# Expert slots of a two-layer diffusion backbone: from four of 128 rows to three, expert 0 at 64 rows and first

## The chip, the cores and the metric

The kernel runs on one core of a Trainium2 chip. The metric is the time of one execution on the device in microseconds (us). The engines are called as in the profile: PE is the matrix engine (PEld its weight loads), DVE the vector engine, ACT the scalar engine, POOL the general one, and SP issues the weight transfers.

## What is computed

A backbone of two layers works on 256 latent and 256 context tokens of width 1024. Each layer mixes the tokens and then applies a feed-forward part: a dense SwiGLU in the first layer, and in the second one a mixture of eight SwiGLU experts for the 256 latent tokens, two experts per token. The change touches the experts alone:

```python
def swiglu(h, w_gate, w_up, w_down):
    return (jax.nn.silu(h @ w_gate) * (h @ w_up)) @ w_down

def moe_swiglu(h, router_w, w_gate, w_up, w_down):
    logits = (h @ router_w).astype(F32)
    top_v, top_i = lax.top_k(logits, TOP_K)
    top_w = jax.nn.softmax(top_v, axis=-1)
    combine = jnp.sum(jax.nn.one_hot(top_i, N_EXPERTS, dtype=F32) * top_w[..., None], axis=-2)
    out = jnp.zeros(h.shape[:-1] + (w_down.shape[-1],), h.dtype)
    for e in range(N_EXPERTS):
        out = out + combine[..., e:e + 1].astype(h.dtype) * swiglu(h, w_gate[e], w_up[e], w_down[e])
    return out
```

The gate and up matrices are 1024 x 2816, the down matrix 2816 x 1024, all float32. With the reference's own inputs (seed 0) its router gives experts 0 to 7 these numbers of tokens: 58, 99, 56, 77, 60, 69, 36, 57.

## The kernel before

The last stage of the kernel works through eight **slots**. A slot s is one expert's work for at most `CAPS[s]` rows (tokens), and `RANKS[s]` says which expert it takes: experts are ranked on the chip by their numbers of tokens, most first, and expert 0 is put at rank 0 whatever its number (L1080). So slot 0 always holds expert 0, with 128 rows; slots 2, 4, 6 hold ranks 1 to 3 with 128 rows; slots 1, 3, 5, 7 hold ranks 4 to 7 with 64 rows. Tokens over a slot's rows are counted in `most`; if there are any, a branch at the end (L1343) runs all eight experts once more for them.

Every slot streams one expert's weights in 33 transfers of 1 MB (`load`, issued by SP): 22 for gate and up in six groups of columns, then 11 for down. The buffers are used in turn: three of `wpool`, four of the pool `mo`, and three pieces of the tiles `own` and `whole`, ten in all.

- A 128-row slot (`expert`) splits each half of a transfer into a high and a low part (`split`: ACT L346, then DVE L347) and does three matmuls of 512 columns for each 128 x 512 block: L1196 to L1198 for gate and up, L1232 to L1234 for down.
- A 64-row slot (`expert64`) splits nothing. It uses the float32 weights as they are and puts two matmuls side by side in the array: L1253 for gate and up, L1289 for down. After each group SiLU (ACT L1259), a product (DVE L1260) and transposes (PE L1265, `turned`) make the operand of the down part.

Slots go in pairs that share their selection of tokens. `pick` makes a matrix `oh` of zeros and ones on DVE (L1140). `gather` multiplies the normalised tokens `hn` with it, 32 matmuls of 192 columns (128 for the one slot and 64 for the other) on PE (L1147), and evacuates them on ACT and DVE to `xg` (128 rows, in two parts) and `xs` (64 rows). `scatter_rows` (L1167, L1169) makes the way back, and `scatter` (L1305, L1308) adds a slot's result to the tokens, half of it late, in the next slot. The pair's 128-row slot comes first, and the next pair's gather runs inside the down part of the 64-row slot (`early`). Ahead of slot 0 stand, one after the other, positions and counts (L1059 to L1072), the ranking on DVE (L1078 to L1113), `pick` and the first gather.

Engines run their instructions in the order in which a scheduler put them, so a waiting instruction holds those behind it on its engine.

Of the kernel before, what the change touches and what calls it, by code (L numbers as in the profile page):

```python
# [20 lines left out]
KD = 8  # L21
# [18 lines left out]
RANKS = (0, 4, 1, 5, 2, 6, 3, 7)  # L40
CAPS = (128, 64, 128, 64, 128, 64, 128, 64)
# [40 lines left out]
def host_layout(x, c, ctx, c_ctx, ada_w, ada_b, mix_norm_w, ffn_norm_w, w_in, hg_lb_logits, hg_norm_w,  # L82
# [101 lines left out]
    "slots": (3, 5, 8),  # L184
# [12 lines left out]
def tile_kernel(ctx: ExitStack, tc: tile.TileContext, xT, cT, cR, ada_w, w_in, w_br, w_out, ffn_gu, ffn_d, router,  # L197
# [117 lines left out]
    more = {"pool": None, "raw": 0, "sp": 0, "own": []}  # L315
# [5 lines left out]
    def take(kind, base):  # L321

        turn[kind] += 1
        own = more["own"] if kind == "raw" else []
        return wpool if turn[kind] % (base + more[kind] + len(own)) < base else more["pool"]

    def load(ap, n=2048):
        if more["own"]:
            j = turn["raw"] % (3 + more["raw"] + len(more["own"]))
            if j in PLAN["slots"]:  # L330
                turn["raw"] += 1
                r = more["own"][PLAN["slots"].index(j)]
                nc.sync.dma_start(r[:, :n], ap)
                return r
        p = take("raw", 3)
        r = p.tile([P, 2048], F32, tag="raw", name=nm("raw"), bufs=3 if p is wpool else more["raw"])
        nc.sync.dma_start(r[:, :n], ap)
        return r
# [725 lines left out]
    for t in range(2):  # L1064
        for q in range(2):
# [3 lines left out]
            V.scalar_tensor_tensor(lv, pqs[2 * t + q], r, hv.bitcast(F32), ALU.mult, ALU.subtract)  # L1069
    pp = pm((P, 3, NE))  # L1070
# [46 lines left out]
    xg = mt((2, KD, P), "xg", 1, F32R)
    whole = hpool.tile([P, 2, 2048], F32, tag="hhi", name="whole")
    xs = whole[:, 0, :512].rearrange("p (k c) -> p k c", k=KD)
    a64 = whole[:, 0, 512:].rearrange("p (g q c) -> p g q c", g=6, q=2)  # L1120
    more_buffers(mo, *PLAN["moe"])
    own = hpool.tile([P, 2, 2048], F32, tag="hlo", name="own")
    more["own"] = [own[:, 0], whole[:, 1], own[:, 1]]
    home = {}

    def home_of(s_):

        if s_ == 0:
            return 0
        if s_ not in home:  # L1130
            home[s_] = nc.values_load(num_i[0:1, s_:s_ + 1], engines=[mybir.EngineType.SP], min_val=0, max_val=NE - 1,
                                      skip_runtime_bounds_check_because="clamped to 0..7 before it is stored")
        return home[s_]

    def pick(pr):
        oh = mt((2, 2, P), "oh", 1, F32R)
        for t in range(2):
            for ee in range(2):
                e = 2 * pr + ee
                V.tensor_scalar(oh[:, t, ee], iota64 if ee else iota, pos_s[:, t, e:e + 1], sel_s[:, t, e:e + 1],  # L1140
                                ALU.is_equal, ALU.mult)
        return oh

    def gather(k, oh, turns):
        pg = pm()[:, :192]
        for n, (s_, t) in enumerate(PARTS):
            T.matmul(pg, hn[s_][:, t, k * P:(k + 1) * P], oh[:, t].rearrange("p e s -> p (e s)")[:, :192],  # L1147
                     start=n == 0, stop=n == 3)
        x = tpool.tile([P, 512], F32, tag="tmp", name=nm("x"))[:, :P]
        with tc.high_priority():  # L1150
            for o, src in ((x, pg[:, :P]), (xs[:, k], pg[:, P:])):
                if turns and k % 2:
                    V.tensor_scalar(o, src, a2[:, k, 0:1], sh2[:, k, 0:1], ALU.mult, ALU.add)
                else:
                    S.activation(o, src, AF.Identity, scale=a2[:, k, 0:1], bias=sh2[:, k, 0:1])
            S.activation(xg[:, 0, k], x, AF.Copy)
            V.tensor_tensor(xg[:, 1, k], x, xg[:, 0, k].bitcast(F32), ALU.subtract)

# [15 lines left out]
    def expert(e, oh, st, choose, early):  # L1174
        pr, ee = divmod(e, 2)
        at_ = home_of(e)
        if ee:
            return expert64(e, at_, oh, st, choose, early)
        xv = [xg[:, s_] for s_ in range(2)]
        aT, turn_ = [], []  # L1180
        for g in range(6):
# [57 lines left out]
    def expert64(e, at_, oh, st, choose, early):  # L1239


        aT, turn_ = {}, []
        for g in range(6):
# [3 lines left out]
            for u in range(2):  # L1247
                for c in range(8 // kc):
                    raw = load(moe[at_, 4 * g + 2 * u + c if g < 5 else 20 + u]).rearrange("p (k c) -> p k c", k=kc)
                    for k in range(kc):  # L1250
                        kk = kc * c + k
                        for h_ in range(2):
                            T.matmul(ps[64 * h_:64 * h_ + 64, u, :hw], xs[:, kk], raw[:, k, h_ * hw:(h_ + 1) * hw],  # L1253
# [8 lines left out]
            def turned(a=a, g=g, nt=hw // P):  # L1262
# [3 lines left out]
                o = a64[:, g]  # L1266
# [28 lines left out]
    def scatter(e, h_, pd, ws, oT):  # L1295
# [5 lines left out]
        for m in range(0, 4, 2):  # L1301
# [34 lines left out]
    more["own"] = []  # L1336
# [6 lines left out]
    with tc.If(n_most > 0):  # L1343
        for e in range(NE):
            oh = mt((2, P), "oh", 1)
            shp = mt((2,), "ws", 2)
            V.tensor_scalar(shp, pos[:, :, e], cape[:, e:e + 1], None, ALU.subtract)
            for t in range(2):
                V.tensor_scalar(oh[:, t], iota, shp[:, t:t + 1], sel[:, t, e:e + 1], ALU.is_equal, ALU.mult)
            xe = hpool.tile([P, KD, P], F32, tag="hhi", name=nm("xe"))  # L1350
            for k in range(KD):
                pg = pm()
                for n, (s_, t) in enumerate(PARTS):
                    T.matmul(pg[:, :P], hn[s_][:, t, k * P:(k + 1) * P].bitcast(F32), oh[:, t],
                             start=n == 0, stop=n == 3)
                S.activation(xe[:, k], pg[:, :P], AF.Identity, scale=a2[:, k, 0:1], bias=sh2[:, k, 0:1])
# [88 lines left out]
```

## Time and profile before

| | us |
|---|---|
| three runs: lowest, median, highest | 2143.81, 2148.07, 2153.55 |
| the profiled execution, its own time | 2144.67 |
| its span in the profile | 2142.8 |
| PE busy in the span | 2049.2 (96%) |
| DVE, ACT busy | 1304.7 (61%), 928.2 (43%) |
| expert slots, first matmul to last down matmul | 1441.83 to 2127.34 |

The span is the time from the first to the last instruction in the profile; the execution's own time is 1.9 us longer. Busy time of PE counts matmuls whose ends are modelled, so it is read together with the idle time ahead of its instructions. Times in the views are counted from the span's start.

### The profile page before, as it was taken

The page shows a single profiled execution, that of the slowest core. Times are in us where ns is not written, and L with a number is a line of the kernel's source. Part 1 is how long each engine was busy: PE and PEld are TensorE (multiplying, and loading weights), DVE is VectorE, ACT ScalarE, POOL GpSimd, SP SyncE. Part 2 cuts the span into 40 slices and gives each one's busy share as a digit, 9 for nine tenths or more (in the row PEclk, how much of TensorE's full clock was granted, in tenths as well). Part 3 has the DMA queues.
Part 4 walks back from the last instruction along what each step waited for, and adds up shares of the span by engine and source line. Part 5 has one row for each costly group of instructions (what it writes and reads, how often), then busy time and mean ns, then how long its engine had stood idle before and what let it go on. Part 6 is the DMA issues. An engine that isn't in the chain of part 4 may idle for free.

```text
span 2142.8 us, 34452 instructions
## 1 busy us (share of the span) xinstructions
PE 2049.2 (96%) x13828; PEld 1578.5 (74%) x13828; DVE 1304.7 (61%) x2363; ACT 928.2 (43%) x1427; POOL 35.3 (2%) x101
## 2 busy tenths in 40 slices
PE   6999999999989999999999999989999999999997
PEld 3777777777868878887778888878757856865863
DVE  6667457764455468634777777669618707915941
ACT  3653234323334222223755443348527616715831
POOL 0001000000000000000000000000000000000000
PEclk9999999999999999999999999989999999999999
DMA  8341423112262346322333222369999999999996
GB/s 322 107 168 70 158 79 118 41 61 79 103 250 98 132 162 250 137 68 81 113 122 119 99 104 93 142 240 351 369 421 421 381 419 418 370 398 420 378 382 257
DMA packets 66984, 455.36 MB, mean 213 GB/s; under 512 B 7681, under 2 KB 8193, under 8 KB 13953
## 3 DMA queue, kind: packets, MB, share of 16 engines
q1 hardware_dynamic: 64080, 447.58, 54.3%
q10 hardware_dynamic: 2736, 5.51, 0.8%
q8 instruction: 111, 1.82, 0.3%
q14 instruction: 57, 0.46, 0.1%
HBM read 452.01 MB, written 1.05 MB: 211 GB/s over the span
## 4 chain that ended last, share of the span: by engine, by line
PE 89%; DVE 4%; ACT 4%; DMA 2%; issue 1%; SPq 0%; DVEq 0%; ACTq 0%
PE pj L353 15%; PE pj L354 15%; PE pj L355 15%; PE pj L1253 7%; PE pm L1289 4%; PE pm L1234 2%; PE pm L1232 2%; PE pm L1233 2%; PE pj L1196 2%; PE pj L1197 2%; PE pj L1198 2%; PE pm L590 1%; PE pa L798 1%; PE pm L373 1%; PE po L1198 1%
## 5 line engine op out<-in xcount | busy, mean ns | idle before, releaser
L346 ACT ACTIVATE whi<-raw 128x1024 fp32r<-128x1024 f32 (+3 forms) x442 | 436.1, 993 | 563.6 <-PE pj L354 480.3
L347 DVE TENSOR_TENSOR wlo<-raw,whi 128x1024 fp32r<-128x1024 f32 (+3 forms) x442 | 497.6, 1140 | 207.4 <-ACT whi L346 196.9
L353 PE MATMUL pj<-hhi,whi 128*128 128x512 f32 (+1 forms) x1216 | 452.3, 373 | 11.0 <-ACT hhi L482 8.5
L355 PE MATMUL pj<-hhi,wlo 128*128 128x512 f32 (+1 forms) x1216 | 450.6, 371 | 0.4 <-DVE wlo L347 0.4
L354 PE MATMUL pj<-hlo,whi 128*128 128x512 f32 (+1 forms) x1216 | 449.6, 370 | 0.1
L353 PEld LDWEIGHTS pj<-hhi,whi 128*128 128x128 f32 x1216 | 231.3, 190 | 52.4 <-ACT hhi L482 11.6
L354 PEld LDWEIGHTS pj<-hlo,whi 128*128 128x128 f32 x1216 | 231.2, 190 | 38.4 <-issue 2.3
L355 PEld LDWEIGHTS pj<-hhi,wlo 128*128 128x128 f32 x1216 | 230.9, 190 | 37.9 <-issue 2.5
L1253 PE MATMUL pj<-raw,whole 128*64 128x256 f32 (+1 forms) x1088 | 114.4, 362 | 0.0
L1260 DVE TENSOR_TENSOR act<-act,pj 128x256 f32<-128x256 f32 (+1 forms) x24 | 9.6, 399 | 156.6 <-ACT act L1259 156.6
L1253 PEld LDWEIGHTS pj<-raw,whole 128*64 128x64 f32 x1088 | 73.6, 137 | 33.1 <-issue 2.5
L1259 ACT ACTIVATE act<-pj 128x256 f32<-128x256 f32 (+1 forms) x24 | 8.8, 366 | 144.3 <-PE pj L1253 144.3
L353 PE MATMUL pj<-yhi,whi 128*128 128x512 f32 (+1 forms) x192 | 66.7, 350 | 3.4 <-ACT yhi L508 3.1
L355 PE MATMUL pj<-ahi,wlo 128*128 128x512 f32 x176 | 69.2, 393 | 0.8 <-DVE wlo L347 0.8
L353 PE MATMUL pj<-ahi,whi 128*128 128x512 f32 x176 | 69.1, 393 | 0.0
L1232 PE MATMUL pm<-whi,ahi 128*128 128x512 f32 x176 | 69.0, 392 | 0.0
L1197 PE MATMUL pj<-whi,xg 128*128 128x512 f32 (+1 forms) x192 | 68.8, 359 | 0.0
L1233 PE MATMUL pm<-whi,alo 128*128 128x512 f32 x176 | 68.6, 390 | 0.0
L354 PE MATMUL pj<-alo,whi 128*128 128x512 f32 x176 | 68.5, 389 | 0.0
L1196 PE MATMUL pj<-whi,xg 128*128 128x512 f32 (+1 forms) x192 | 68.4, 356 | 0.1
L1234 PE MATMUL pm<-wlo,ahi 128*128 128x512 f32 x176 | 68.2, 390 | 0.0
L1198 PE MATMUL pj<-wlo,xg 128*128 128x512 f32 (+1 forms) x192 | 68.1, 354 | 0.0
(364 smaller groups left out, 3613.8 us busy)
## 6 DMA issues: line engine op xcount, KB each, us to landing
raw<-in_moe_dram SPq DMA_DIRECT2D x185, 1024.0 KB, 8.8
raw<-in_w_in_dram SPq DMA_DIRECT2D x58, 1024.0 KB, 4.9
own<-in_moe_dram SPq DMA_DIRECT2D x53, 1024.0 KB, 9.0
raw<-in_ada_w_dram SPq DMA_DIRECT2D x44, 1024.0 KB, 5.0
whole<-in_moe_dram SPq DMA_DIRECT2D x26, 1024.0 KB, 8.6
raw<-in_ffn_gu_dram SPq DMA_DIRECT2D x22, 1024.0 KB, 4.8
raw<-in_w_br_dram SPq DMA_DIRECT2D x12, 1024.0 KB, 4.9
raw<-in_ffn_d_dram SPq DMA_DIRECT2D x16, 704.0 KB, 4.1
```

Of the source, the lines that this page charges most:

```text
L346: S.activation(hi, src, AF.Copy)
L347: V.tensor_tensor(lo, src, hi.bitcast(F32), ALU.subtract)
L353: T.matmul(ps, whi(k), hhi(k), start=first and k == 0, stop=False)
L354: T.matmul(ps, whi(k), hlo(k), start=False, stop=False)
L355: T.matmul(ps, wlo(k), hhi(k), start=False, stop=last and k == n - 1)
L1196: T.matmul(ps[:, :w], xv[0][:, kk], hi[:, k], start=kk == 0, stop=False)
L1197: T.matmul(ps[:, :w], xv[1][:, kk], hi[:, k], start=False, stop=False)
L1198: T.matmul(ps[:, :w], xv[0][:, kk], lo[:, k], start=False, stop=kk == 7)
L1232: T.matmul(pd[h_], ahi, hi[:, k % 2], start=first, stop=False)
L1233: T.matmul(pd[h_], alo, hi[:, k % 2], start=False, stop=False)
L1234: T.matmul(pd[h_], ahi, lo[:, k % 2], start=False, stop=last)
L1253: T.matmul(ps[64 * h_:64 * h_ + 64, u, :hw], xs[:, kk], raw[:, k, h_ * hw:(h_ + 1) * hw], start=u + kk == 0, stop=u == 1 and kk == 7, tile ...
```

## The change

Slots become `CAPS = (128, 64, 128, 64, 128, 64, 64, 64)` with `RANKS = (1, 0, 2, 4, 3, 5, 6, 7)`. Expert 0 is slot 1, with 64 rows; ranks 1 to 3 are slots 0, 2 and 4, with 128 rows; ranks 4 to 7 have 64 rows. In each pair the odd slot runs first, so the order is 1, 0, 3, 2, 5, 4, 7, 6. Slot 1 uses the unranked `pos` and `sel` of expert 0, and its gather (64 columns) is written ahead of the counts and the ranking; the gather of slot 0 (128 columns) stands inside slot 1, after its first group. Later gathers run in the down part of the pair's 128-row slot, and `scatter_rows` is done in the odd slot.

The 64-row operands move into columns of `xts` and `cm` that are no longer used. That frees a piece of `whole`, so there are eleven buffers, in a fixed ring (`mmmmwww0123`: four of `mo`, three of `wpool`, four pieces). A fourth PSUM tile for the transposed tokens comes from the group `pj`, where before it waited for one of the three `pm` tiles. The branch for left-over tokens now asks for each expert whether it has any.

```diff
-RANKS = (0, 4, 1, 5, 2, 6, 3, 7)
-CAPS = (128, 64, 128, 64, 128, 64, 128, 64)
+RANKS = (1, 0, 2, 4, 3, 5, 6, 7)
+CAPS = (128, 64, 128, 64, 128, 64, 64, 64)
...
-    pqs = [pm((P, 4, P)) for _ in range(4)]
+    pqs = [pm((P, 4, P)) for _ in range(3)]
 
     def rows_of(m):
+        if m == 4:
+            pqs.append(pj((P, 4, P)))
...
+    xs = [xts[k // 4][:, 64 * (k % 4):64 * (k % 4) + 64] for k in range(KD)]
+    xs2 = [cm[:, 64 * k:64 * k + 64] for k in range(KD)]
+    a64 = [xts[2 + g][:, :256].rearrange("p (q c) -> p q c", q=2) for g in range(6)]
...
+    more.update(own=[own[:, 0], whole[:, 0], own[:, 1], whole[:, 1]], ring=PLAN["ring"])
...
+                ps_, se, o = (pos, sel, 0) if RANKS[e] == 0 else (pos_s, sel_s, e)
...
+    ohs = [pick(0, (1,))]
+    for k in range(KD):
+        gather(0, k, ohs[0], (1,), True)
     pp = pm((P, 3, NE))
     T.matmul(pp[:, 2], onev, sel[:, 0], start=True, stop=False)
...
-        for ee in range(2):
-            def choose():
-                if ee and pr < 3:
+        for ee in (1, 0):
+            def choose(g):
+                if ee and pr + g == 0:
+                    pick(0, (0,), ohs[0])
+                    for k in range(KD):
+                        gather(0, k, ohs[0], (0,))
+                if ee and g == PLAN["sg"]:
+                    st.update(zip(("ws", "oT"), scatter_rows(pr, ohs[pr])))
+                if not ee and pr < 3 and g == PLAN["pk"]:
                     ohs.append(pick(pr + 1))
 
             def ahead(k):
-                if ee and pr < 3 and 0 <= k < KD:
-                    gather(k, ohs[pr + 1], False)
+                if not ee and pr < 3 and 0 <= k < KD:
+                    gather(pr + 1, k, ohs[pr + 1])
...
+            n_rest = nc.values_load(rest_i[0:1, e:e + 1], min_val=0, max_val=256)
+            with tc.If(n_rest > 0):
+                tokens_left(e)
```

**PE ahead of the first slot.** Before (rows left out at "..." are more of the gather, L1147):

```order
L1059 MATMUL pm_13067<-sel_13054,cc 128x16
L1060 MATMUL pm_13067<-sel_13054,onev 128x8
L1071 MATMUL pm_13081<-sel_13054,onev 128x8
L1072 MATMUL pm_13081<-sel_13054,onev 128x8
L1147 MATMUL pm_13133<-oh_13128,hn_2119_13071 128x192
...
L1196 MATMUL po_13213<-whi_13216,xg_13125 128x512
```

With the change (L1110 is the gather, L1129 and L1130 the counts, L1263 the gate and up matmuls of a 64-row slot, eight for a transfer; at the first "..." stand gathers, at the second two more transfers of L1263, at the third more of the gather of 128 columns):

```order
L1060 MATMUL pm_13067<-sel_13054,cc 128x16
L1061 MATMUL pm_13067<-sel_13054,onev 128x8
L1110 MATMUL pm_13087<-oh_13084,hn_2119_13071 128x64
...
L1129 MATMUL pm_13135<-sel_13054,onev 128x8
L1130 MATMUL pm_13135<-sel_13054,onev 128x8
L1263 MATMUL pj_13181<-raw_13182,x_5578 64x256 x8
...
L1263 MATMUL pj_13181<-raw_13212,x_5580 64x256 x8
L1110 MATMUL pm_13227<-oh_13084,hn_2119_13071 128x128 x2
...
L1263 MATMUL pj_13299<-raw_13300,x_5578 64x256 x8
```

The counts, and with them the ranking, moved behind the gather of expert 0; the second gather moved into the first slot.

**PE in a down part with a gather.** Before it was that of a 64-row slot (L1289; L1147 is the gather, L1265 a transpose of the last group):

```order
L1289 MATMUL pm_14367<-whole 64x512 x4
L1147 MATMUL pm_14376<-oh_14271,hn_2119_13071 128x192 x2
L1147 MATMUL pm_14376<-oh_14271,hn_2120_13072 128x192 x2
L1265 MATMUL pm_14386<-cc,act_14364 128x128
L1289 MATMUL pm_14367<-raw_14374,whole 64x512 x4
```

With the change it is that of a 128-row slot (L1242 to L1244, on split weights `whi` and `wlo`):

```order
L1244 MATMUL pm_14225<-wlo_14279,ahi_13856 128x512
L1110 MATMUL pm_14290<-oh_14040,hn_2119_13071 128x192 x2
L1110 MATMUL pm_14290<-oh_14040,hn_2120_13072 128x192 x2
L1242 MATMUL pm_14225<-whi_14300,ahi_13956 128x512
L1243 MATMUL pm_14225<-whi_14300,alo_13957 128x512
L1244 MATMUL pm_14225<-wlo_14301,ahi_13956 128x512
```

The gather's four matmuls for each of eight blocks moved from between unsplit weights to between split ones.

**PE in the first group of a 64-row slot** (four transfers to a group). Before, in slots 3, 5 and 7, the transposes of the group (L1265) follow its own last matmuls:

```order
L1253 MATMUL pj_16748<-whole 64x256 x8
L1253 MATMUL pj_16748<-raw_16758,whole 64x256 x8
L1253 MATMUL pj_16748<-raw_16768,whole 64x256 x8
L1253 MATMUL pj_16748<-own,whole 64x256 x8
L1265 MATMUL pm_16801<-cc,act_16787 128x128 x2
```

With the change, in slots 1, 3, 5 and 7, one transfer of the next group (another `pj`) stands between them:

```order
L1263 MATMUL pj_15906<-raw_15907,x_5578 64x256 x8
L1263 MATMUL pj_15906<-raw_15917,x_5580 64x256 x8
L1263 MATMUL pj_15906<-raw_15927,x_5578 64x256 x8
L1263 MATMUL pj_15906<-raw_15937,x_5580 64x256 x8
L1263 MATMUL pj_15950<-raw_15951,x_5578 64x256 x8
L1275 MATMUL pm_15961<-cc,act_15947 128x128 x2
```

Counted over a slot's first five groups in this order, transposes that follow their own group's last matmul are 2 in slot 1 and 5 in each of slots 3, 5 and 7 before (17); now they are none in slot 1, 3 in each of slots 3, 5 and 7, and 5 in slot 6 (14).

## Rows read from the trace of the kernel before

**Rows 1.** The page, chain of waits that ended last, by engine.

```profile
PE 89%; DVE 4%; ACT 4%; DMA 2%; issue 1%; SPq 0%; DVEq 0%; ACTq 0%
```

**Rows 2.** Windows, slots 0 to 7: us, PE, PEld, DVE, ACT, POOL, PEclk, DMA, GB/s.

```profile
1441.83:1538.03 96.20, 96.06 (x464) 79.26 (x462) 86.73 (x92) 73.86 (x82) 0.00 (x0) 1.00 0.90 340
1538.03:1610.74 72.71, 69.01 (x533) 38.79 (x532) 10.23 (x26) 14.94 (x41) 0.00 (x0) 1.00 1.00 413
1610.74:1707.79 97.05, 96.53 (x470) 80.35 (x470) 88.57 (x92) 74.43 (x79) 0.00 (x0) 1.00 1.00 404
1707.79:1783.52 75.73, 69.21 (x532) 38.82 (x531) 10.32 (x26) 14.93 (x41) 0.00 (x0) 1.00 1.00 414
1783.52:1882.15 98.63, 98.10 (x471) 81.56 (x471) 88.67 (x92) 74.42 (x79) 0.00 (x0) 0.98 0.98 386
1882.15:1957.88 75.73, 69.21 (x532) 38.77 (x532) 10.33 (x26) 14.93 (x41) 0.00 (x0) 1.00 1.00 411
1957.88:2056.43 98.55, 98.02 (x471) 81.43 (x471) 87.66 (x88) 74.41 (x79) 0.00 (x0) 0.98 0.98 383
2056.43:2127.34 70.91, 65.81 (x508) 36.50 (x507) 7.31 (x16) 7.61 (x19) 0.00 (x0) 1.00 0.89 363
```

**Rows 3.** Timeline of PE, slot 7: start, us, what, [idle before <-releaser].

```profile
2086.53 1.90 PE L1253 MATMUL pj<-whole 128*64 128x256 f32 x16
...
2091.09 0.44 PE L1265 MATMUL pm<-cc,act 128*128 128x128 f32 x2 [0.94 <-DVE act L1260]
```

**Rows 4.** Groups of PE by line and shape, 1428 us to the end.

```profile
L1147 PE MATMUL pm<-oh,hn 128*128 128x192 f32 x128 | 24.0, 318 | 5.3 <-DVE most L1111 4.9
...
L1265 PE MATMUL pm<-cc,act 128*128 128x128 f32 x44 | 9.9, 299 | 16.0 <-DVE act L1260 16.0
...
L1169 PE MATMUL pm<-cc,oh 128*128 128x128 f32 x16 | 4.7, 307 | 0.0
...
L1167 PE MATMUL pm<-by,oh 128*128 128x1 f32 x32 | 4.5, 209 | 0.0
```

**Rows 5.** Windows: slot 7 until its last transfer is in; 100 us in slots 1 and 2.

```profile
2056.43:2121.40 64.97, 59.87 (x482) 34.66 (x482) 7.31 (x16) 7.61 (x19) 0.00 (x0) 1.00 0.97 396
1555.00:1655.00 100.00, 95.77 (x590) 63.63 (x587) 48.29 (x64) 48.01 (x74) 0.00 (x0) 1.00 1.01 421
```

**Rows 6.** Timeline of PE ahead of slot 0.

```profile
1428.54 0.58 PE L1059 MATMUL pm<-sel,cc 128*128 128x16 f32 x2 [2.21 <-issue]
1428.95 0.57 PE L1060 MATMUL pm<-sel,onev 128*128 128x8 f32 x2
...
1435.24 6.76 PE L1147 MATMUL pm<-oh,hn 128*128 128x192 f32 x32 [4.85 <-DVE most L1111]
```

**Rows 7.** Timeline of DVE ahead of slot 0.

```profile
1429.57 0.17 DVE L1061 TENSOR_SCALAR pos<-pm 128x16 f32<-128x16 f32 x1 [0.85 <-PE pm L1060]
...
1434.23 0.34 DVE L1140 TENSOR_SCALAR oh<-cc,by,by 128x128 fp32r<-128x128 f32 x1
```

**Rows 8.** Timeline of ACT: a gather's three evacuations.

```profile
1436.83 0.46 ACT L1155 ACTIVATE x<-pm,mods,coef 128x128 f32<-128x128 f32 x1 [9.68 <-PE pm L1147]
1437.19 0.40 ACT L1155 ACTIVATE whole<-pm,mods,coef 128x64 f32<-128x64 f32 x1
1437.48 0.31 ACT L1156 ACTIVATE xg<-x 128x128 fp32r<-128x128 f32 x1
```

**Rows 9.** Windows of 5 us: two with idle time of PE; a stretch in slot 4.

```profile
1425.00:1430.00 5.00, 2.55 (x11) 2.21 (x12) 3.75 (x14) 1.25 (x3) 0.00 (x0) 0.50 1.00 423
...
2080.00:2085.00 5.00, 4.06 (x36) 2.41 (x34) 0.42 (x1) 0.77 (x2) 0.00 (x0) 1.00 1.01 421
...
1784.82:1788.23 3.41, 3.41 (x8) 2.76 (x9) 2.85 (x3) 1.60 (x2) 0.00 (x0) 0.50 1.02 423
```

More of the change, by code (lines that the diff above doesn't have):

```diff
@@ L183 @@
     "td": 2,
-    "slots": (3, 5, 8),
+    "ring": "mmmmwww0123",
     "pk": 3,
@@ L312, in tile_kernel @@
     lb_v, lb_n = lb[:, 2], lb[:, 3]
-    more = {"pool": None, "raw": 0, "sp": 0, "own": []}
+    more = {"pool": None, "raw": 0, "sp": 0, "own": [], "ring": ""}
     turn = {"raw": 0, "sp": 0}
@@ L323, in take @@
         turn[kind] += 1
-        own = more["own"] if kind == "raw" else []
-        return wpool if turn[kind] % (base + more[kind] + len(own)) < base else more["pool"]
+        return wpool if turn[kind] % (base + more[kind]) < base else more["pool"]
     def load(ap, n=2048):
[L328 to L336, printed above, removed]
+        if more["ring"]:
+            kind = more["ring"][turn["raw"] % len(more["ring"])]
+            turn["raw"] += 1
+            p = {"w": wpool, "m": more["pool"]}.get(kind)
+            r = more["own"][int(kind)] if p is None else None
+        else:
+            p, r = take("raw", 3), None
+        if r is None:
+            r = p.tile([P, 2048], F32, tag="raw", name=nm("raw"), bufs=3 if p is wpool else more["raw"])
         nc.sync.dma_start(r[:, :n], ap)
@@ new lines, in tile_kernel, with home_of @@
+    own = hpool.tile([P, 2, 2048], F32, tag="hlo", name="own")
+    more_buffers(mo, *PLAN["moe"])
+    more.update(own=[own[:, 0], whole[:, 0], own[:, 1], whole[:, 1]], ring=PLAN["ring"])
+    turn["raw"] = 0
+    home = {}
+    def home_of(s_):
+        if RANKS[s_] == 0:
+            return 0
+        if s_ not in home:
+            home[s_] = nc.values_load(num_i[0:1, s_:s_ + 1], engines=[mybir.EngineType.SP], min_val=0, max_val=NE - 1,
+                                      skip_runtime_bounds_check_because="clamped to 0..7 before it is stored")
+        return home[s_]
@@ L1117, in tile_kernel @@
[L1117 to L1133, printed above, removed]
@@ L1135, in pick @@
-    def pick(pr):
-        oh = mt((2, 2, P), "oh", 1, F32R)
-        for t in range(2):
-            for ee in range(2):
[L1139 to L1157, printed above, removed]
+    V.tensor_copy(rest_i, cnt_)
@@ L1213, in expert @@
             turn_.append(turned)
-            if g == PLAN["pk"]:
-                choose()
+            choose(g)
             if g == PLAN["sg"]:
-                if late:
-                    late.pop()()
-                st.update(zip(("ws", "oT"), scatter_rows(pr, oh)))
+                late.pop()()
         pd = [pm(), pm()]
@@ L1319, in tile_kernel @@
     norm = Norm(256, lambda: pt("po", 1))
-    late, ohs = [], [pick(0)]
-    for k in range(KD):
-        gather(k, ohs[0], True)
+    late = []
     for pr in range(4):
         st = {}
-        for ee in range(2):
-            def choose():
-                if ee and pr < 3:
+        for ee in (1, 0):
[7 more added lines that the diff above has]
+                if not ee and pr < 3 and g == PLAN["pk"]:
@@ L1344, in tile_kernel @@
         for e in range(NE):
[L1345 to L1356, printed above, removed]
@@ L1387, in tile_kernel @@
-            pd = [pm(), pm()]
-            for c in range(11):
-                raw = load(moe[e, 22 + c]).rearrange("p (k c) -> p k c", k=4)
-                for k in range(4):
-                    h_, kk = DOWN[4 * c + k]
-                    first, last = (kk == 0, kk == 21) if h_ == 0 else (kk == 20, kk == 19)
-                    T.matmul(pd[h_], ae[:, kk], raw[:, k], start=first, stop=last)
-            y = mt((2, 512), "y")
-            for h_ in range(2):
-                S.activation(y[:, h_], pd[h_], AF.Copy, scale=ws[:, 0:1])
@@ L1397, in tile_kernel @@
-            yf = y.rearrange("p a b -> p (a b)")
-            ov = oT.rearrange("p t c -> p (t c)")
-            for m in range(KD):
-                ps = pm()
-                T.matmul(ps[:, :256], yf[:, m * P:(m + 1) * P], ov, start=True, stop=True)
-                V.scalar_tensor_tensor(xl[m], ps[:, :256], mods[1][:, 40 + m, 0:1], xl[m], ALU.mult, ALU.add)
+            n_rest = nc.values_load(rest_i[0:1, e:e + 1], min_val=0, max_val=256)
+            with tc.If(n_rest > 0):
+                tokens_left(e)
```

147 lines of the change are left out of this document (101 added, 46 removed).

## The prediction

> **What bounds the kernel now.** I read the chain of waits that ended last first: 89% of the span lies on PE and 2% on transfers [rows 1]. That is an average over stages, so the windows of the eight slots come next [rows 2]. Look at three columns there. PE: in each slot its busy time fills the window but for a few us. DVE and ACT: 87 to 89 and 74 us in a 128-row slot, about 10 and 15 in a 64-row slot. GB/s: 383 to 414 in slots 1 to 6. So a 128-row slot lasts 96 to 99 us for 33 transfers, a 64-row slot 71 to 76.
>
> How fast can transfers come? In 100 us with no hole they ran at 421 GB/s [rows 5]. A transfer is 1024 x 256 float32 or as many elements in another shape, 1.0486 MB, so 2.49 us each and 82 us for a slot's 33. A 128-row slot (2.9 to 3.0 us a transfer on PE) is slower than that, a 64-row slot (2.15 to 2.3) faster, and lives on what the ten buffers hold. Slots now alternate, so PE never runs dry. The idle time that PE does have is of one kind: 0.94 us ahead of a transpose, for the product on DVE [rows 3], 16.0 us over the stage [rows 4], 17 times.
>
> Where the trace is silent: no two 64-row slots follow each other, no gather stands between split matmuls, none is 64 columns wide.
>
> **The change, term by term.** I sum by pairs of slots, because the gather and `scatter_rows` only move within a pair or between its members. All is set against the profiled execution's own time, 2144.67; the median of the runs is 3.4 above that.
>
> *First three pairs.* Each stays one 128-row and one 64-row slot: 168.9, 172.8 and 174.4 us by the windows [rows 2]. The gather's matmuls move from a 64-row to a 128-row slot at the same cost on PE. Its evacuations move too: 0.46 + 0.40 + 0.31 = 1.17 us of ACT for each of eight blocks [rows 8]. ACT has 74 busy us of 97 there, so 9.4 more fit on average; and PE spends 4 x 0.18 = 0.72 us of each block on the gather itself, during which the next splits can run. I cost this at nothing; cover gone, it is a rival below. What changes for certain is the order of transposes: of 17 gaps 14 stay, and those of the first three pairs fall from 12 to 6 (slots 3 and 5 have 3 each, slot 1 none). 6 x 0.94 = **-5.6 us**.
>
> *Last pair.* It was 98.55 + 70.91 = 169.5 us [rows 2]; now both slots have 64 rows. PE's work: 2 x 70.91 plus `scatter_rows`, 16 matmuls of 4.7 us and 32 of 4.5 over four pairs [rows 4], so 2.3 a pair: 144.1. In this pair the gaps go from 5 in slot 7 to 5 in slot 6 and 3 in slot 7; 2 x 70.91 holds ten of them, so two go, -1.9: 142.2 us if PE never waits for weights.
>
> The transfers are slower than that. In the old slot 7 they ran 64.97 us at 396 GB/s until the last one was in [rows 5]: 25.7 MB or 24.5 transfers. So 8.5 of the 33 were in when it began, of ten buffers, and 24.5 x 2.49 = 61.0 leaves 4.0 us of holes. Now 66 transfers are wanted and eleven buffers put some 9.5 ahead, because the slot before the pair still has 128 rows and lets the ring fill. 56.5 x 2.49 + 4.0 = 144.7 us until the last one is in; its own matmuls take about 1.9 [rows 3]: 146.6. PE catches up with the transfers late in the second slot and waits some 4 us in all. 146.6 - 169.5 = **-22.9 us**.
>
> What the chip's memory gives is the number on which this rests. The rows say 421 GB/s over 100 us, 414 over a whole slot. The Trainium skill (DMA: Bandwidth & Descriptors, "Where 436 GB/s comes from") holds that in a transfer from memory into the on-chip buffer the memory side, some 358 GB/s, is what limits a core. By that figure 56.5 transfers would take an estimated 165.5 us and the pair 171.4, so the whole term would be lost, and the sum would be 2142. The trace disagrees with that for one core working alone [rows 2, 5]; I go by the trace.
>
> *Start.* Before, PE counts, waits 4.85 us for the ranking on DVE, gathers 192 columns in 6.76 us [rows 6], and slot 0 begins at 1441.83. Now expert 0 needs no rank: positions are out at 1429.57 + 0.17 = 1429.74, two picks at 0.34 follow [rows 7], and a gather of 64 columns can begin at 1430.4. The price of its 32 matmuls isn't shown. From above it is 6.76, that of 192 columns; from below a third of it, 2.3. The later gathers took (24.0 - 6.76)/96 = 0.18 us a matmul [rows 4, 6], in place of 0.21; I take 0.18, since for small shapes the duration hardly falls with the columns (209 ns for one column, 307 for 128 [rows 4]): 5.8 us, to 1436.2. The two count matmuls cost some 0.9 us (0.58 and 0.57 for their like, which overlap a little [rows 6]); the first slot begins at 1437.1, 4.7 earlier. The ranking then runs on DVE under a slot that leaves it idle. But the gather of 128 columns now stands inside that slot, another 32 x 0.18 = 5.8 us that was part of the 6.76 before. Together **+1 us**, between -5 (both gathers priced by columns) and +3.
>
> The clock could add to it. Between 1425 and 1430, PE busy for 2.55 of 5 us, the granted clock was 0.50, which is 1.2 of 2.4 GHz [rows 9]. The new start leaves PE less idle, which if anything helps.
>
> *Nothing.* The fourth tile of transposes moves ahead of the stage where PE is not held by it; the branch per expert adds eight tests of a number at the end in place of one, on engines that are done, below 1 us each, and no more than 1 to 2 us if they come one after the other: it is in the range. The eleventh buffer is in the term above.
>
> Sum: -22.9 - 5.6 + 1 = -27.5; 2144.67 - 27.5 = 2117.2, and 2120.6 if set against the median. I give **2118 us**.
>
> **The rivals.**
>
> *PE never waits (2113).* If the transfers' 4.0 us of holes vanish because eleven buffers in a fixed ring keep them fed, the pair takes 142.6, PE's own time or nearly: 4 us less. For it: 421 GB/s held over 100 us. Against it: the old slot 7, whose buffers were also free early, had the holes.
>
> *The evacuations hold the splits (2128).* ACT and DVE work through their queues in order, and the splits of the next weights stand behind a gather's evacuations. 1.17 us of ACT against 0.72 of PE leaves 0.45 us a block; 8 blocks in 3 slots make 10.7, so 2128. Fully exposed it is 3 x 9.4 = 28 us, and the gain is gone. For it: DVE is busy 87 of 97 us in such a slot [rows 2], and takes a part of these evacuations. Against it: PE has other split weights waiting in that time.
>
> *Transfers stay slow (2131).* With no 128-row slot in the pair the holes may not close: at the 383 GB/s of slot 6 [rows 2], 2.74 us each, 56.5 of them take 154.8, the pair 160.7, and the time is 2131. The skill's rule above would stand here, at 2142, with a small chance.
>
> *Slower: the clock halves.* In the last two slots PE waits for weights again and again. In a stretch where the granted clock was 0.50, eight 128 x 512 matmuls took 3.41 us, 0.43 each, against 96.53/470 = 0.21 in slot 2 [rows 2, 9]. With all of the last pair at that clock PE would need 284 us instead of 142, and the kernel 2255. The gain of 27.5 is used up once 32 us of the pair's work run at half clock (the first 4.4 lie under the wait for transfers). Against it: between 2080 and 2085 PE was busy for 4.06 of 5 us, and the clock stayed at 1.00 [rows 9]; waiting for weights would leave it busy for 1.9 of 2.49, which is as much to the eye. For it: the 0.50 at 2.55 of 5. The Trainium skill (TensorE: Matmul & The Clock Gate, "HAM oscillation — how this bites in real kernels") tells of just such a kernel, slowed to a half by waits for transfers between bursts of matmuls.
>
> *The branch for left-over tokens is taken (2215).* Expert 0 has 64 rows whatever its number. By the reference's counts it has 58, so 6 more would be needed; the branch decides at the 65th token and costs at least one expert's transfers, 33 x 2.49 = 82 us, and a second time what follows the slots, 2142.8 - 2127.3 = 15.5 us by the table of times.
>
> **How the numbers follow.** The forecast has 0.56, PE-bound 0.17, held splits 0.18, slow transfers 0.04, half clock 0.04, the branch 0.01. What a measurement of this kernel can tell from no change is about 0.5%, 10.7 us: faster means below 2137.3. That holds for the first three, and part of the fourth and of the clock's case: 0.91; within 0.5% 0.04; slower 0.05. The range reaches from 2105 (2113 with the start at its best end, -6, and 2 for the profile's distance) to 2131 (held splits and the start's bad end), which leaves out the rest.
>
> **What would show it.** Slot 1 first, beginning near 1437. Slots of 128 rows as long as before, with no idle time of PE ahead of L1242 where the gather stands. The last two slots together near 147 us, with PE's idle time ahead of L1263 or L1298 put down to transfers, only in the second slot; the transfers at 415 GB/s or more over both. The granted clock at 1.00 there. I would be wrong if the last pair took over 155 us, if gaps of PE after each gather add up to more than 5 us, or if the clock fell to 0.50.

## The result and the profile after

The changed kernel takes 2124.95 us (median of four runs, 2120.40 to 2126.47), beside 2147.41 before (also four runs): ratio 0.9889, with a 95% interval of 0.9861 to 0.9916, a gain of 22.5 us or 1.1%. The forecast was 2118 in 2105 to 2131. The profiled execution is the slowest of the four, 2126.47, with a span of 2124.7.

The chain of waits that ended last, by engine, in the kernel after, answers to [rows 1]:

```profile
PE 84%; DMA 6%; DVE 5%; ACT 3%; issue 2%; SPq 0%; DVEq 0%; ACTq 0%
```

Transfers went from 2 to 6% of the span. The windows of its slots, in the order 1, 0, 3, 2, 5, 4, 7, 6, and then of what follows them, answer to [rows 2] (same columns):

```profile
1437.88:1511.38 73.50, 71.03 (x537) 40.45 (x536) 13.84 (x54) 12.73 (x33) 0.00 (x0) 0.96 0.91 369
1511.38:1614.05 102.67, 102.15 (x491) 84.06 (x491) 89.91 (x95) 80.12 (x102) 0.00 (x0) 0.98 0.99 402
1614.05:1684.89 70.84, 65.90 (x512) 36.70 (x511) 9.16 (x23) 8.05 (x18) 0.00 (x0) 1.00 0.99 409
1684.89:1787.68 102.79, 102.26 (x490) 84.11 (x490) 89.88 (x95) 80.14 (x102) 0.00 (x0) 0.98 0.98 393
1787.68:1858.53 70.85, 65.90 (x513) 36.70 (x512) 9.17 (x23) 8.05 (x18) 0.00 (x0) 1.00 1.00 411
1858.53:1961.12 102.59, 102.06 (x490) 84.22 (x490) 88.34 (x87) 78.69 (x94) 0.00 (x0) 0.98 0.98 392
1961.12:2029.27 68.15, 64.93 (x512) 36.48 (x513) 7.37 (x17) 6.37 (x15) 0.00 (x0) 1.00 1.00 412
2029.27:2106.52 77.25, 67.61 (x509) 36.00 (x505) 7.30 (x16) 7.62 (x19) 0.00 (x0) 1.00 0.96 397
2106.52:2124.69 18.17, 5.07 (x17) 3.24 (x16) 5.66 (x13) 3.22 (x7) 0.00 (x0) 0.68 0.19 63
```

Read it by pairs. The last pair took 145.4 us where it had been 169.5. In its second slot PE is busy for 67.6 of 77.3 us, with the clock at 1.00: it waits for weights. Two of its waits (PE: start, us, what, idle before):

```profile
2071.30 1.95 PE L1263 MATMUL pj<-whole,cc 128*64 128x256 f32 x16 [0.54 <-DMA whole<-in_moe_dram]
...
2083.73 1.94 PE L1298 MATMUL pm<-raw,x 128*64 128x512 f32 x8 [0.55 <-DMA raw<-in_moe_dram]
```

Such waits add up to 4.1 us there; in the pair's first slot there is none. The other pairs got longer or hardly shorter: 176.2, 173.6 and 173.4 against 168.9, 172.8 and 174.4. And each 128-row slot shows a clock of 0.98.

The chain through the last pair, in order of time (start, us, what; pieces under 5 us left out):

```profile
2009.76 5.33 PE pm L1298 x24
...
2015.10 16.41 DMA raw<-in_moe_dram
...
2031.62 19.76 DMA raw<-in_moe_dram
...
2051.50 19.76 DMA whole<-in_moe_dram
...
2071.38 19.77 DMA raw<-in_moe_dram
...
2101.22 5.33 PE pm L1298 x24
```

A transfer takes 19.8 us from issue to landing here: eight are in flight, and they land 2.49 us apart. From 2015 to 2091 the chain holds nothing but transfers and their issue. From the pair's start to the last landing, and from there to the last down matmul (windows, columns of [rows 2]):

```profile
1961.12:2103.55 142.43, 129.56 (x1007) 71.76 (x1008) 14.67 (x33) 13.99 (x34) 0.00 (x0) 1.00 1.00 412
2103.55:2106.52 2.97, 2.97 (x14) 0.72 (x10) 0.00 (x0) 0.00 (x0) 0.00 (x0) 1.00 0.00 0
```

142.4 + 3.0 = 145.4, where the sum had 144.7 + 1.9 = 146.6.

Now the entry into a 128-row slot, here slot 2. First ACT, then PE (start, us, what, idle before):

```profile
1683.21 0.69 ACT L1308 ACTIVATE y<-pm,ws 128x512 fp32r<-128x512 f32 x1 [11.06 <-PE pm L1298]
1683.80 2.94 ACT L345 ACTIVATE whi<-raw 128x1024 fp32r<-128x1024 f32 x3
```

```profile
1684.89 0.50 PE L1209 MATMUL po<-whi,xg 128*128 128x512 f32 x1 [1.73 <-ACT whi L345]
...
1686.15 0.61 PE L1211 MATMUL po<-wlo,xg 128*128 128x512 f32 x1 [0.53 <-DVE wlo L346]
1686.56 0.63 PE L1209 MATMUL po<-whi,xg 128*128 128x512 f32 x1
```

ACT idles for 11 us at `y`, the late half of the 64-row slot's result, which needs PE's last down matmul; the splits of the next weights stand behind it. PE then waits twice, and its matmuls take 0.63 us in place of 0.39, as the granted clock has fallen to 0.50. The same gaps, 1.73 and 0.53 us, were in the kernel before at the entries of slots 2, 4 and 6; the granted clock fell behind two of them there, behind all three now.

The start of the experts on PE:

```profile
1428.40 0.58 PE L1060 MATMUL pm<-sel,cc 128*128 128x16 f32 x2 [5.03 <-issue]
...
1430.13 7.01 PE L1110 MATMUL pm<-oh,hn 128*128 128x64 f32 x32 [0.74 <-DVE oh L1102]
...
1437.88 8.46 PE L1263 MATMUL pj<-raw,x 128*64 128x256 f32 x64
1446.28 2.45 PE L1110 MATMUL pm<-oh,hn 128*128 128x128 f32 x20
```

The gather of 64 columns takes 7.0 us, all of it at clock 0.50; that of 192 columns took 6.8 [rows 6], most of it at 0.50. In that state the matmuls of both start 213 ns apart (median), so their count sets the price, not their width. The gather of slot 0's 128 columns stands at 1446, inside slot 1.

### The profile page after: what moved, and what is told of

Same layout as the page of the kernel before. It is cut to its first block, busy times and chain, and to the rows that moved or that the text cites. A ratio compares the mean times of both kernels' runs of the same rounds, so it can differ in the third digit from the quotient of the medians.

```text
span 2124.7 us, 34306 instructions
## 1 busy us (share of the span) xinstructions
PE 2029.1 (96%) x13901; PEld 1542.2 (73%) x13901; DVE 1220.6 (57%) x2280; ACT 856.1 (40%) x1357; POOL 35.3 (2%) x101
## 4 chain that ended last, share of the span: by engine, by line
PE 84%; DMA 6%; DVE 5%; ACT 3%; issue 2%; SPq 0%; DVEq 0%; ACTq 0%
PE pj L352 15%; PE pj L353 15%; PE pj L354 14%; PE pj L1263 8%; PE pm L1298 3%; DMA raw<-in_moe_dram 3%; PE pm L1242 1%; PE pm L589 1%; PE pm L1244 1%; PE pm L1243 1%; PE pj L1210 1%; PE pj L1211 1%; PE pj L1209 1%; DVE wlo L346 1%; PE pm L372 1%
## 5 line engine op out<-in xcount | busy, mean ns | idle before, releaser
L345 ACT ACTIVATE whi<-raw 128x1024 fp32r<-128x1024 f32 (+2 forms) x382 | 372.9, 982 | 544.8 <-PE pj L353 479.9
L346 DVE TENSOR_TENSOR wlo<-raw,whi 128x1024 fp32r<-128x1024 f32 (+2 forms) x382 | 426.4, 1127 | 211.3 <-ACT whi L345 206.5
L352 PEld LDWEIGHTS pj<-hhi,whi 128*128 128x128 f32 x1216 | 231.4, 191 | 53.6 <-ACT hhi L481 12.5
L353 PEld LDWEIGHTS pj<-hlo,whi 128*128 128x128 f32 x1216 | 231.4, 190 | 38.3 <-issue 2.3
L1263 PE MATMUL pj<-raw,x 128*64 128x256 f32 x896 | 104.1, 389 | 0.0
L1263 PEld LDWEIGHTS pj<-raw,x 128*64 128x64 f32 x896 | 64.1, 140 | 34.6 <-issue 5.4
L1309 DVE SCALAR_TENSOR_TENSOR y<-pm,ws,y 128x512 fp32r<-128x512 f32 x16 | 12.0, 750 | 98.4 <-ACT y L1308 98.4
L1298 PE MATMUL pm<-raw,x 128*64 128x512 f32 x280 | 64.1, 597 | 3.1 <-DMA raw<-in_moe_dram 3.1
L353 PE MATMUL pj<-ylo,whi 128*128 128x512 f32 (+1 forms) x192 | 66.3, 346 | 0.0
L354 PE MATMUL pj<-yhi,wlo 128*128 128x512 f32 (+1 forms) x192 | 66.2, 345 | 0.0
L1242 PE MATMUL pm<-whi,ahi 128*128 128x512 f32 x132 | 52.8, 400 | 0.0
L1308 ACT ACTIVATE y<-pm,ws 128x512 fp32r<-128x512 f32 x16 | 10.9, 684 | 103.2 <-PE pm L1298 93.1
```

The source lines that it names most:

```text
L345: S.activation(hi, src, AF.Copy)
L346: V.tensor_tensor(lo, src, hi.bitcast(F32), ALU.subtract)
L352: T.matmul(ps, whi(k), hhi(k), start=first and k == 0, stop=False)
L353: T.matmul(ps, whi(k), hlo(k), start=False, stop=False)
L354: T.matmul(ps, wlo(k), hhi(k), start=False, stop=last and k == n - 1)
L1242: T.matmul(pd[h_], ahi, hi[:, k % 2], start=first, stop=False)
```

## The experiments

All ran beside the kernel before on the same chip. Ratios are to the kernel before; the changed kernel's is 0.9889. The slots are compared by their lengths in the profiled executions: the work ahead of the experts, which only experiment 7 touches, ended anywhere from 1417.2 to 1423.1 us there, so whole times of two kernels can differ by some us for that alone.

**1. Slot 6 back to 128 rows** (`four128`).

```diff
-CAPS = (128, 64, 128, 64, 128, 64, 64, 64)
+CAPS = (128, 64, 128, 64, 128, 64, 128, 64)
```

> Slot 6 back to 128 rows (rank 6 gets them, after slot 7), everything else as in the changed kernel: this undoes the last pair's term alone. Theory (the last pair is where the time came from): the pair goes from 145.4 to some 168 to 170 us (64-row slot near 68, 128-row slot near 100, without a gather in it), and the end comes 23 to 25 us later: some 2149, no better than before the change, so that everything else in the change is worth nothing or less together. Rival (the order, the start and the buffers have a share in the gain): some 2138.

Measured: 2147.29 us, ratio 1.0004 (0.9990 to 1.0018). The last pair of `four128`, windows:

```profile
1959.64:2029.69 70.05, 65.10 (x512) 36.33 (x511) 8.14 (x19) 8.06 (x18) 0.00 (x0) 1.00 1.00 408
2029.69:2129.09 99.40, 98.87 (x466) 80.81 (x466) 87.93 (x87) 75.21 (x82) 0.00 (x0) 1.00 0.73 304
```

169.45 us against 145.40: 24.1 us, and the whole gain is gone. So the last pair accounts for the gain, and order, start, buffers and transposes together are worth nothing that can be measured.

**2. Eight buffers in place of eleven** (`ring8`).

```diff
-    "ring": "mmmmwww0123",
+    "ring": "mmmmwww0",
```

> The ring of buffers cut from eleven to eight (the last three pieces are not used); nothing else. Theory (the last pair is bound by transfers, so each buffer fewer is one transfer fewer ahead when the pair begins): 3 x 2.49 = 7.5 us later, some 2132, with PE's waits for transfers in the last pair starting in the first of its two slots. Rival (PE's own work bounds the pair, or the fixed order of the ring is what keeps the transfers fed): no change, 2125, or a loss spread over all slots.

Measured: 2136.35 us, ratio 0.9962 (0.9948 to 0.9976). The windows of slot 1 and of the last pair:

```profile
1431.94:1509.21 77.27, 71.89 (x536) 40.28 (x535) 13.83 (x54) 12.72 (x33) 0.00 (x0) 0.96 0.91 372
1958.37:2029.29 70.92, 65.75 (x513) 36.17 (x512) 7.38 (x17) 6.88 (x16) 0.00 (x0) 1.00 1.00 410
2029.29:2111.70 82.41, 69.19 (x507) 35.27 (x507) 7.31 (x16) 7.11 (x19) 0.00 (x0) 1.00 0.96 398
```

The last pair takes 153.3 us, 7.9 more for three transfers at 2.49 (7.5): 7 of its 66 transfers had landed when it began, and 10 in the changed kernel. So each buffer is worth one transfer there: transfers bound it. Another 3.8 us lie in slot 1, 77.3 against 73.5. PE waits 2.0 us for transfers in it, and not at all in the changed kernel; the rest was not traced. The theory had left slot 1 out.

**3. A fifth slot of 64 rows** (`two128`).

```diff
-CAPS = (128, 64, 128, 64, 128, 64, 64, 64)
+CAPS = (128, 64, 128, 64, 64, 64, 64, 64)
...
-    n_most = nc.values_load(most_i[0:1, 0:1], min_val=0, max_val=256)
```

> One more slot, 4, cut to 64 rows. Its expert has 69 tokens in the reference's inputs, so five of them are left out, and the branch for left-over tokens with them; four 64-row slots then stand at the end. Theory (transfers bound a row of 64-row slots): from the start of slot 5 132 transfers less 9.5 that are in, at 2.49 us, plus 4.0 + 1.9, are 311 us, where the changed kernel takes 319: only 8 us gained, some 2117, with PE waiting in the last three slots. Rival (PE bounds them): slot 4 falls from 102.6 to some 74 us, 28 us gained, some 2097.

This kernel leaves out five tokens and the branch, so only its time is of use. Measured: 2114.61 us, ratio 0.9866 (0.9847 to 0.9886). Slots 5, 4, 7, 6:

```profile
1782.33:1851.28 68.95, 65.73 (x513) 36.89 (x513) 8.39 (x21) 6.37 (x15) 0.00 (x0) 1.00 1.00 408
1851.28:1928.88 77.60, 70.24 (x533) 38.30 (x530) 7.22 (x16) 11.57 (x31) 0.00 (x0) 1.00 1.01 421
1928.88:2011.93 83.05, 68.64 (x512) 35.33 (x512) 7.38 (x17) 6.57 (x16) 0.00 (x0) 1.00 1.01 421
2011.93:2094.53 82.60, 69.16 (x507) 35.22 (x507) 7.30 (x16) 7.11 (x19) 0.00 (x0) 1.00 0.94 392
```

312.2 us, forecast 311, and 6.6 less than the same four slots of the changed kernel; PE's rival had 28 us of gain. From the third slot on, a 64-row slot costs 83 us, with PE busy for 69 of them, and 33 x 2.49 = 82. The change has taken the last cheap step: a further slot of 64 rows gains some 7 us, not 24.

**4. The splits ahead of the late half** (`splits_first`). `wt` is a copy of `ws` that also reads the third split, so ACT's `y` can't be ordered ahead of it.

```diff
-                late.pop()()
+                late.pop()(his[2])
...
+        if hi is not None:
+            w2 = mt((2,), "wt")
+            V.scalar_tensor_tensor(w2, hi[:, 0, :2].bitcast(F32), 0.0, ws, ALU.mult, ALU.add)
+            ws = w2
```

> The late half of a 64-row slot's result (ACT's y, L1308) is made to depend on the third split of the 128-row slot that follows, so ACT makes three splits ahead of it. In the changed kernel ACT stands at y until PE's last down matmul, with the splits behind it: PE waits 1.73 + 0.53 us at each of three entries into a 128-row slot, and the granted clock is 0.50 for some 3.4 us right behind each. Theory (the queue order of ACT makes the gap, and the gap makes the clock fall): both gaps go and the clock stays at 1.00 there: 3 x (2.26 + 1.6) = 11.6 us, some 2113. Rival 1 (the clock falls for another reason): only 6.8 us, some 2118. Rival 2 (PE has more time than the transfers, which become the bound): the gain is taken back by waits for transfers in the last two slots, some 2122.

Measured: 2112.97 us, ratio 0.9857 (0.9831 to 0.9883). The entry of slot 0 and the three 128-row slots:

```profile
1503.40:1509.40 6.00, 6.00 (x28) 3.85 (x25) 4.93 (x6) 3.88 (x4) 0.00 (x0) 1.00 1.02 422
1505.17:1606.10 100.93, 100.72 (x493) 82.98 (x491) 88.76 (x96) 79.22 (x102) 0.00 (x0) 1.00 1.01 417
1675.14:1776.06 100.92, 100.71 (x492) 82.97 (x490) 87.17 (x94) 78.74 (x101) 0.00 (x0) 1.00 1.00 407
1845.11:1945.83 100.72, 100.51 (x493) 83.04 (x491) 85.66 (x86) 77.34 (x93) 0.00 (x0) 1.00 1.00 407
```

For the same six us around the entry of slot 0 the changed kernel has:

```profile
1509.64:1515.64 6.00, 3.75 (x10) 2.75 (x10) 4.47 (x5) 4.58 (x5) 0.00 (x0) 0.72 1.01 421
```

No gap and no fall. 12.0 us are gained by the medians, and 10.9 in the traces from the end of the normalisation to the last down matmul, where 11.6 were expected. The queue order on ACT made the gap. With the gap gone the clock fell at none of the 12 entries in this kernel and the three later ones that keep the edit (`both`, `align256`, `warm`). In the eight kernels with the gap it fell at 15 of 24 entries: two of three before, three of three in the changed kernel, one of three in `align`. So the falls hang on the gap, but a gap does not always bring one.

**5. Addresses** (`align`, `both`, `align256`, `before_pad`). In the 128-row slots of the changed kernel 128 x 512 matmuls follow each other at 233.1 ns on average, by their starts in the trace; before at 228.0. (Means over pairs that start less than 300 ns apart, at clock 1.00.) A new tile of 32 bytes (`rest_i`) and the order of allocation had moved `xg`, one pair of `whi` and `wlo`, and `ahi` and `alo` from 128 modulo 256 to addresses of 32 modulo 64. No trace holds addresses: these are counted from the tiles, and what the runs show is what unused tiles of a given size do.

```diff
+    mt((8,), "pad")
     xg = mt((2, KD, P), "xg", 1, F32R)
```

> One unused tile of 32 bytes ahead of xg; nothing else. In the changed kernel a new small tile (rest_i, 32 bytes) and the order of allocation put xg, the split weights, ahi and alo at addresses of 32 modulo 64, where before they were at 0 modulo 64; their 128 x 512 matmuls follow each other at 232 to 233 ns there, at 227 before. Theory (address): the spacing returns to 227 to 228 ns in all three 128-row slots, each is some 1.8 us shorter (near 101 us), and the end comes 5 us earlier, some 2120; the output's transfer, from a tile of the same pool, may lose its extra 1.5 us too. Rival (the gather or the ring of eleven buffers disturbs the reading of the operands): the spacing stays at 232 to 233, and the time stays at 2125.

> The unused tile and the splits ahead of y, together. If both theories hold and do not meet: 2125 - 5 - 11.6, some 2108 (2106 to 2111). If the last two slots are bound by transfers and these start no earlier than PE frees their buffers, both gains still count, because they shift the start of the last pair. If either theory falls, the sum falls by its part.

Measured: `align` 2121.55 us, ratio 0.9894 (0.9869 to 0.9918); `both` 2112.66, ratio 0.9852 (0.9825 to 0.9878), no better than `splits_first`. The spacing went to some 231.4 ns in both, a third of the way, and the slots of `both` are only 0.5 us shorter. As stated, the theory (multiples of 64 suffice) fell. So the addresses were put back modulo 256, with `pad` of 96 bytes and two more:

```diff
+    mt((24,), "pad")
...
+    mt((32,), "pad2")
...
+                mt((48,), "pad3")
```

> The splits ahead of y, and unused tiles of 96, 128 and 192 bytes that put xg, the four weight buffers, whi, wlo, ahi and alo of this pool at the same addresses modulo 256 as in the kernel before (128). With 32 bytes alone, 0 modulo 64, the spacing of the 128 x 512 matmuls came from 233.0 to 231.3 ns, not to the 227.6 of before. Theory (a coarser alignment, or where operands lie against each other modulo 256, makes the rest): the spacing goes to 227 to 229 ns and each 128-row slot from 100.9 to some 99 us: some 2107. Rival (something else in these slots: the ring's order of writes, the gather's work on ACT): the spacing stays near 231, some 2112.

Measured: 2109.35 us, ratio 0.9844 (0.9824 to 0.9863); spacing 229.1 ns, 227 in the median. The slots:

```profile
1505.35:1605.04 99.69, 99.39 (x492) 82.80 (x490) 88.59 (x96) 79.41 (x102) 0.00 (x0) 1.00 1.01 420
1674.08:1773.78 99.70, 99.40 (x493) 82.80 (x491) 86.89 (x94) 78.84 (x101) 0.00 (x0) 1.00 1.00 413
1842.82:1942.34 99.52, 99.22 (x493) 82.90 (x491) 85.36 (x86) 77.35 (x93) 0.00 (x0) 1.00 1.00 412
```

1.2 us a slot shorter than in experiment 4. The interval of its ratio overlaps that of experiment 4, so the slots show the gain and the whole times do not. And the opposite, in the kernel before:

> The kernel before, with one unused tile of 32 bytes ahead of xg, so that its xg, whi, wlo, ahi and alo lie at 32 modulo 64 as in the changed kernel; nothing else. Theory (addresses): the spacing of the 128 x 512 matmuls in its four 128-row slots goes from 227.6 to some 233 ns, 420 matmuls a slot, so each slot is some 1.8 to 2.2 us longer and the end some 8 us later: 2153. Rival (the addresses matter only together with the new ring or the new order): the spacing stays, 2145.

Measured: spacing 232.2 ns. Two of its 128-row slots, without a fall of the clock:

```profile
1439.49:1536.90 97.41, 97.34 (x464) 79.31 (x463) 86.93 (x92) 73.84 (x82) 0.00 (x0) 1.00 0.90 336
...
1959.62:2058.10 98.48, 97.95 (x470) 80.61 (x471) 87.92 (x88) 74.47 (x79) 0.00 (x0) 1.00 0.99 387
```

They are 1.2 us longer than slot 0 and 1.4 longer than slot 2, the fellows without a fall in [rows 2]. The whole time hardly moved: 2146.89 us, ratio 1.0007 (0.9996 to 1.0018). The expected 8 us were too much: by the trace it is 1.2 to 1.4 us in each of four slots, 5 to 6 in sum, and even that is more than the interval allows (3.9). The profiled execution had one fall of the clock in place of two; that, 1.6 us, covers a part. Shown: tiles that nothing uses move the spacing, in both kernels and both ways, and in the kernel before one such tile is the only edit, so where the tiles lie is the cause. Not settled: which operand it is, and how much of it the whole time keeps.

**6. The ranked start** (`ranked_start`): counts, ranking, one gather of 192 columns, then slot 1.

```diff
-    ohs = [pick(0, (1,))]
-    for k in range(KD):
-        gather(0, k, ohs[0], (1,), True)
...
+    ohs = [pick(0)]
+    for k in range(KD):
+        gather(0, k, ohs[0], (0, 1), True)
```

> The start put back: counts, ranking, one gather of 192 columns for both slots, and then slot 1; no gather inside slot 1. In the changed kernel slot 1 begins 4 us earlier than slot 0 did before, but 4.7 us of gather stand inside it, its first 3.5 us run at a granted clock of 0.50, and in the profiled execution the clock fell once more behind that gather. Theory (the start is worth nothing): slot 1 begins some 4 us later and is 4.7 us plus 1.7 of clock shorter, the end comes 0 to 3 us earlier: 2122 to 2125. Rival (an earlier first slot is a gain that lasts): 4 us later, some 2129.

Measured: 2118.47 us, ratio 0.9879 (0.9860 to 0.9898). Its slot 1:

```profile
1437.26:1503.35 66.09, 63.95 (x504) 35.77 (x504) 8.82 (x25) 8.81 (x22) 0.00 (x0) 1.00 0.97 396
```

Counted from PE's last matmul of the normalisation, slot 1 begins 3.7 us later and is 7.4 shorter, at full clock from its first matmul. In the trace the slots end 2.6 us earlier by that count; the rival's 4 us later is excluded. In these two traces the unranked start loses a little; the intervals of the two ratios overlap.

**7. PE kept busy ahead of the first slot** (`warm`, on top of `align256`).

```diff
+    warm = pj()
+    for i in range(16):
+        T.matmul(warm[:, :256], ident, xl[7], start=True, stop=True)
```

> The version with the splits ahead of y and the operands at 128 modulo 256, and 16 matmuls of 128 x 256 whose result nobody reads, in PE's idle time behind the normalisation ahead of the experts (they need the last block of tokens, so they come neither earlier nor much later). There the granted clock is 0.50 from some 1423 to 1439 us: the 64-column gather takes 6.8 us at it, and slot 1's first 2 to 3 us. Theory (the clock falls for the 5 us in which PE is idle): the clock stays at 1.00, the gather takes some 3.5 us, slot 1 begins some 3 us earlier and is 1.5 us shorter: 4 to 5 us, some 2105. Rival (the clock falls all the same, or the matmuls delay the counts): 2109 to 2111.

Measured: 2107.26 us, ratio 0.9829 (0.9815 to 0.9842), the lowest of all, though its interval overlaps that of `align256`. PE at its start, most of the added matmuls (L1040; the 16 stand as 32 in the trace) and the gather (L1114):

```profile
1420.61 5.43 PE L1040 MATMUL pj<-x,cc 128*128 128x256 f32 x24
...
1427.42 4.19 PE L1114 MATMUL pm<-oh,hn 128*128 128x64 f32 x32
...
1432.36 9.69 PE L1269 MATMUL pj<-raw,x 128*64 128x256 f32 x64
```

The gather takes 4.2 us in place of 7.0. But the clock fell again, from some 1431 to 1437.5 us, in that gather and with PE busy without a pause. From the end of the normalisation to the last down matmul 2.9 us were won in the trace, not 4 to 5.

## Why the prediction was right, term by term

Predicted against measured, in the two profiled executions (us):

| | predicted | measured |
|---|---|---|
| first slot begins | 1437.1 | 1437.9 |
| first pair, with a gather of 5.8 | 172.8 | 176.2 |
| second pair | 170.9 | 173.6 |
| third pair | 172.5 | 173.4 |
| last pair | 146.6 | 145.4 |
| behind the slots | 15.4 | 18.2 |
| end of the span | 2115.3 | 2124.7 |

- **The last pair, -22.9: right, -24.1**, and for the reason given. Experiments 1 to 3 show it from three sides: undone, it costs 24.1; a buffer is a transfer; a fifth slot meets the transfers' 83 us. Of the 66 transfers, 10 had landed when it began (9.5 forecast). The 421 GB/s on which it rested held: from the 13th of the 66 to the last they landed 2.49 us apart. The holes ahead of that were some 3 us (4.0 forecast), and PE's waits 4.1 us (some 4). One sign was missed: with these holes the pair ran at 412 GB/s to its last landing, not at 415 or more.
- **No wait behind a gather: right.** In a 128-row slot PE shows no idle time ahead of the down matmuls, and a gather matmul is 0.27 us (groups of PE after, busy, mean ns, idle before):

```profile
L1242 PE MATMUL pm<-whi,ahi 128*128 128x512 f32 x132 | 52.8, 400 | 0.0
...
L1110 PE MATMUL pm<-oh,hn 128*128 128x192 f32 x96 | 14.3, 270 | 0.0
```

- **The transposes, -5.6: right.** 14 gaps of 0.94 us are left in the trace, six fewer than before in the first three pairs and three more in the last one, where they lie beside waits for transfers.
- **"Moves at the same cost", pairs 1 to 3: the term that was mis-sized**, 7 of the 9.4 us that are missing. The sum held that a 128-row slot gains the gather and nothing else. Its matmuls of 512 columns became slower (5.1 ns for each of 372, by the spacing), 1.9 us a slot or 5.7 in three; experiment 5 won 1.2 a slot back. The clock fell at three entries in these pairs where it had fallen at one, 2 x 1.6 = 3.2 us by the difference of slots 4 and 2 in [rows 2]. Against that a gather is cheaper between split matmuls, 4.8 us (14.3 for three) and not 5.7, so -2.9. These make 6.0; the start adds some more in the first pair, below. I had read the 0.98 of slots 4 and 6 in [rows 2], and not asked whether slot 2, with the same gap, would keep its 1.00. And "the idle time that PE does have is of one kind" was wrong: it passed over 1.73 and 0.53 us at each of three entries, 6.8 us in all.
- **The start, +1: the sign was right, the size was not.** The first gather took 7.0 us and the second 4.7, where 5.8 were forecast for each. I let the 0.50 of [rows 9] help, and it moved into slot 1: 2.8 us of slot 1 ran at it, and 3.4 more behind the second gather. By experiment 6 the two cost some 2.7 us, 7.4 less the 4.7 of the gather.
- **Behind the slots, 2.8 us later, not forecast.** The clock fell during the last normalisation (its eight matmuls 3.59 us in place of 2.34), 1.25 us; 1.3 more passed between the last output's landing and the end, 3.3 us against 2.0. In `four128`, with the same branch, it is 2.0 again; what makes it was not tried.
- **The rivals.** Half clock in the last pair: the clock was at 1.00 in both slots, with PE busy for 0.88 of the second. Slow transfers: two of the full slots of experiment 3 ran at 421 GB/s. The branch was not taken; the eight tests that I put in the range stand inside it, so no run shows what they cost.
- **The range.** 2125 lies in it partly by luck. It reached up to 2131 for held splits and a bad start; the splits were not held, and most of the missing time came from the matmuls and the clock in the 128-row slots, which it had not been made for.

## What to carry to other kernels

When two stages alternate between an engine's bound and the transfers' bound, cost a change by the transfers left after what the buffers hold; a stage made faster than its weights arrive is worth only that difference, and the next one of its kind much less (24 us for the first, some 7 for the second here). Look at what an in-order queue puts ahead of the next stage's first step: one evacuation of 0.7 us on ACT cost PE 2.3 us at each entry, and a fall of the clock at most of them, and moving it gave half as much as the whole change. And compare the addresses of the operands when matmuls of one shape get slower with nothing else changed.

## What the runs showed of the hardware

- Matmuls of 128 x 512 followed each other at 227 ns in the median with operands at 128 modulo 256, at 231 with these at other multiples of 64 (`xg` at 64, `whi` at 0 modulo 256), and at 232 with them at 32 modulo 64. The times are from the traces of experiment 5, the addresses counted from the tiles.
- The granted clock fell from 1.00 to 0.50 not only right behind idle time of PE. It fell near the end of the second gather in three of the nine traces that have one (the changed kernel, `four128`, `both`), and PE pauses 0.28 us in that gather in all nine. In `warm` it fell in the first gather, with no pause of PE in the 10 us ahead. The 2 us around the fall, in the changed kernel and in `warm` (columns of [rows 2]):

```profile
1450.00:1452.00 2.00, 1.98 (x14) 1.34 (x14) 0.88 (x3) 1.91 (x7) 0.00 (x0) 0.72 1.04 438
1430.00:1432.00 2.00, 2.00 (x15) 2.00 (x14) 0.69 (x2) 0.77 (x2) 0.00 (x0) 0.69 0.09 33
```

- A gather's price hardly depends on its columns. By their starts (median) its matmuls followed each other at 213 ns for 64 and for 192 columns at clock 0.50, and at 112, 112 and 111 ns for 64, 128 and 192 columns at 1.00. With the pauses between them, 32 matmuls of 64 columns took 7.0 us at 0.50 and 4.2 with the clock at 1.00 for most of it.
